# Placing x, the weights and the k order by their byte distances in SBUF in a two-layer hybrid block

## The chip, the core and the metric

The kernel runs on one core of one Trainium2 chip. The metric is the device time of one execution in microseconds, the median of the runs; the kernel before took 1326.98 us (median of 3 runs, 1326.49 to 1327.44). A smaller time is better.

## The reference

Two layers of a block on 256 tokens of width 1024, with 16 learned meta tokens in front (so T = 272). Each layer normalizes, projects to twelve parts, runs three branches (retention, a gated recurrence hgrn2, differential attention), mixes them through gates, and adds a gated feed-forward with a three-tap convolution:

```python
def mixer(hn, ...):
    proj = (hn @ w_in).astype(F32)                      # 1024 -> 13312
    o_ret = retention(rq, rk, rv, rg, ...); o_hg = hgrn2(...); o_da = diff_attention(...)
    y_b = jnp.einsum('blnc,ncd->blnd', branches, w_branch)   # three 1024x1024
    y = jnp.sum(jax.nn.sigmoid(mg) * y_b, axis=2)
    return y @ w_out                                     # 1024x1024

def conv_ffn(hn, ...):
    u = hn @ w_ffn_in                                    # 1024 -> 5632
    c = conv_b + sum(conv_w[j] * up[:, j:j + l] for j in range(3))
    gate, val = jnp.split(c, 2, axis=-1)
    return (jax.nn.silu(gate) * val) @ w_ffn_out         # 2816 -> 1024

for li in range(2):
    h = h + mixer(rms_norm(h, g_mix), ...)
    h = h + conv_ffn(rms_norm(h, g_ffn), ...)
return rms_norm(h, g_final)[:, PAD:]
```

Nearly all arithmetic is in the products of activations with weights.

## The kernel before, in words

Activations lie with features on the 128 partitions and tokens along them. A weight matrix is cut into tiles of 128 x 128, and one stream holds all tiles of both layers in the order of use. `_Weights.next` (L577) takes the stream in chunks of eight tiles: SP loads 512 KB into `wraw`, ACT copies it to `whi` (rounded to float32r), and DVE writes the remainder `wraw - whi` to `wlo`. Activations are split in the same way into a high and a low part. Each weight tile is then used in three matmuls, in this order (`products`, L873 to L875):

```python
nc.tensor.matmul(o, wh, hi, start=first, stop=False)
nc.tensor.matmul(o, wh, lo, start=False, stop=False)
nc.tensor.matmul(o, wl, hi, start=False, stop=last)
```

The weight tile is the operand that is loaded (128 columns of 4 bytes), the activation tile the one that moves. A moving tile has 272 columns, or 258 in those parts of the second layer that need no row of the meta tokens but the last two ("short"; `t0 = 14` moves its start by 56 bytes). L558 is the helper that records every other operation.

The stages of a layer, with the moving operand:

- **base**: the twelve projections, 52 pairs of output tiles, moving x. Six arrays hold x: `xs[0]`, `xs[1]`, `xs[2]`, each with a high and a low part. k tiles 0 to 3 come from `xs[0]`, or from `xs[2]` once the norm's factor is folded into x (from the fifth pair on), and k tiles 4 to 7 from `xs[1]`. In the second layer 22 of the 52 pairs run on all 272 columns (`FULL`), 30 are short.
- **blocks**: `b0`, `b1`, `b2` and `wo`, 16 pairs; the moving tiles lie in slots of 4 x 272 elements, so that one k tile begins 1088 bytes behind the other.
- **fi**: the feed-forward's first product, 22 pairs, moving x again.
- **fo**: its second product. In the first layer four pairs over 22 k tiles, moving `ghi` and `glo`; the fourth pair (`fo`, 3) takes all k of one output tile and then of the other. In the second layer `final` (L1351) turns the roles round: 512 columns of a weight chunk move, and 128 tokens of `ghi` or `glo` are loaded (L1383 to L1385).

A pair in base, blocks and fi is 8 k tiles x 2 output tiles x 3 = 48 matmuls; k is the outer loop of the two output tiles.

`_places` (L127) puts each weight tile of a chunk at a start that is fixed modulo 256 bytes, by the numbers in `APART` and, for fi, `SPREAD[j]`; gaps are left unused. Where a chunk's tiles don't lie in one run, `_runs` splits ACT's and DVE's work into pieces. What matters below is a **distance**: the start address of the operand that is loaded for the next matmul, less the start of the operand that moves in this one, modulo 256 bytes. By the addresses of the built program it is 64 in base on 272 columns, 104 in short base, 64 + `SPREAD[j]` in fi (another number for each pair), and in blocks and fo 64 (short: 104) but 128 (short: 168) where k goes up, which is one matmul in six.

A planner (`_Plan`) orders all instructions by costs and due times; it knows no addresses. `SLOTS` is the number of slots that it may hand out.

Of the kernel before, what the change touches and what calls it, by code (L numbers as in the profile page):

```python
# [19 lines left out]
P = 128  # L20
DEPTH = 2
# [13 lines left out]
TAIL = T - 2 * P  # L35
BANK = 512
CHUNK_TILES = 8
SLOTS = 13
LEAD = 6.0
MARGIN = 12.0  # L40
EARLY = 12.0
# [42 lines left out]
    return FK if name == "fo" else KD  # L84


def _turns(li):

    pairs = [x for x in ORDER if x[0][0] not in MARKS]
    if li == DEPTH - 1:
        pairs = [x for x in pairs if x[0] != "fo"]
    groups = [[x] for x in pairs]
    if li == 0:
        groups[:2] = [pairs[:2]]
    turned = [[x] for n in (BASE, ("fi",)) for x in [x for x in pairs if x[0] in n][DEFER - 1 : DEFER]]
    out = []
    for group in groups:  # L100
        if group == [("fo", 3)]:
            out.append([("fo", 3, k, f) for f in range(2) for k in range(FK)])
# [24 lines left out]
def _places(depth=DEPTH):  # L127

    wants = []
    for li in range(depth):
        for name, j, k, _ in sum(_turns(li), []):
            if name == "fo" and (li == DEPTH - 1 or j == 3):
                wants.append(None)
                continue
            short = li == DEPTH - 1 and name not in FULL
            if name in BASE or name == "fi":
                wants.append((SPREAD[j] + 4 * T0 * short if name == "fi" else APART[short]) % LINE)
                continue  # L140
            wants.append(APART[short] + BLOCK * (name[0] == "b" or name in ("wo", "fo")) + 64 * (k % 4))
    out = []
    for c in range(0, len(wants), CHUNK_TILES):
        at, places = 0, []
        for want in wants[c : c + CHUNK_TILES]:
            if want is not None:
                at += (want // 4 - at) % (LINE // 4)
            places.append(at)
            at += P
        assert at <= ROOM  # L150
        out.append(places)
    return out


def _runs(places):


    runs = []
    for i, at in enumerate(places):
        if runs and at == runs[-1][1] + runs[-1][2] * P:  # L160
            runs[-1][2] += 1
        else:
            runs.append([i, at, 1])
    out = []
    for i, at, n in runs:
        if out and out[-1][4] == n and (out[-1][3] == 1 or at == out[-1][1] + out[-1][2] * out[-1][3]):
            if out[-1][3] == 1:
                out[-1][2] = at - out[-1][1]
            out[-1][3] += 1
        else:  # L170
            out.append([i, at, 0, 1, n])
    return out


# [20 lines left out]
def _stream(w_in, w_branch, w_out, w_ffn_in, w_ffn_out):  # L195

    out = np.empty((DEPTH, STREAM, P, P), np.float32)
    for li in range(DEPTH):
        tiles = sum(_turns(li), [])
        for i, (name, j, k, f) in enumerate(tiles):  # L200
            if name in BASE:
                w, cols = w_in[li], _columns(name, BASE[name] + 2 * j + f)
            elif name in ("b0", "b1", "b2"):
                w, cols = w_branch[li][int(name[1])], _columns(name, 2 * j + f)
            elif name == "wo":
                w, cols = w_out[li], _columns(name, 2 * j + f)
# [6 lines left out]
    out = out.reshape(n, CHUNK_TILES, P, P).transpose(0, 2, 1, 3)  # L213
    return np.ascontiguousarray(out).reshape(n, P, CHUNK_TILES * P)


# [346 lines left out]
class _Weights:  # L563
# [6 lines left out]
        self.used = 0  # L570
        self.places = _places()

    def part(self, t, at, step, runs, n):

        return bass.AP(t.tensor, t.offset + at, [list(t.ap[0]), [max(step, 1), runs], [1, n * P]])

    def next(self):  # L577
        c, i = divmod(self.used, CHUNK_TILES)
        self.used += 1
        if i == 0:  # L580
# [7 lines left out]
            for p in range(pieces):  # L588
                n = CHUNK_TILES // pieces
                cols = slice(p * n * P, (p + 1) * n * P)  # L590
                self.sp.dma_start(raw[:, cols], self.w[c][:, cols])
                for first, at, step, runs, each in _runs(self.places[c][p * n : (p + 1) * n]):
                    src = raw[:, (p * n + first) * P : (p * n + first + runs * each) * P].rearrange("p (r x) -> p r x", r=runs)
                    self.act.activation(self.part(hi, at, step, runs, each), src, AF.Copy)
                    self.dve.tensor_tensor(out=self.part(lo, at, step, runs, each), in0=src, in1=self.part(hi, at, step, runs, each).bitcast(F32), op=SUB)
            self.plan.key = due
            self.cut = hi, lo
        hi, lo = self.cut
        at = self.places[c][i]
        return hi[:, at : at + P], lo[:, at : at + P]  # L600

    def chunk(self):

# [13 lines left out]
def _trace(ctx, tc, plan, a, depth, probe):  # L617
# [330 lines left out]
    for li in range(depth):  # L948
# [402 lines left out]
        def final():  # L1351
# [21 lines left out]
            for k, t, c in order:  # L1373
# [33 lines left out]
        for name, j in ORDER:  # L1407
# [111 lines left out]
                    norm.finish()  # L1519
            elif name == "fi":  # L1520
                ps = products(lambda k: x_tile(k, norm.folded), name, j, t0)
                if j % 4 == 0:
                    st.setdefault("ghi", []).append(slot4("ghi", F32R))
                    st.setdefault("glo", []).append(slot4("glo", F32R))
                u = ps
                if not norm.folded:
                    u = temp2("two_a")[:, :, t0:]
                    evacuate(u, ps)
                first = META if last else 0
                c = temp2("two_b")  # L1530
                for f in range(2):
                    ft = j + f * FK
# [9 lines left out]
                split(st["ghi"][j // 4][:, j % 4, first:], st["glo"][j // 4][:, j % 4, first:], c[:, 0, :])  # L1542
            elif last:
                if j == 0:
                    final()
# [37 lines left out]
```

## Time and profile before

| | before |
|---|---|
| median of 3 runs | 1326.98 us |
| the profiled execution | 1326.42 us |
| its span | 1324.6 us |
| TensorE matmul busy, matmuls | 1314.0 us, 11862 |
| TensorE weight load busy | 1285.7 us |
| VectorE (DVE) busy | 962.4 us |
| ScalarE (ACT) busy | 816.4 us |
| mean granted TensorE clock | 0.999 |

The span is the time between the first and the last instruction that the profiler saw. Busy times of one engine are sums over the span. A matmul's record lasts longer than the distance to the next one's start, since matmuls are pipelined: in a stretch that begins at a matmul's start, the count of matmuls holds two that had begun ahead of it. The pace of a stretch is therefore its length divided by the count less two.

### The profile page before, as it was taken

What the parts mean: (1) busy time and instruction counts of PE and PEld (TensorE: products, weight loads), DVE (VectorE), ACT (ScalarE), POOL (GpSimd) and SP (SyncE); (2) the same over time, 40 slices, a digit from 0 to 9 for tenths busy, and PEclk for the clock granted to TensorE, in tenths of its full rate; (3) what the DMA queues carried; (4) which work ended last, traced back from release to release, by engine and by line L of the source; (5) the groups of instructions that cost most, each with busy time, mean ns of one, the idle gap of its engine ahead of it and who ended that gap; (6) DMA issues with size and microseconds to landing.
All of it is one profiled execution on the core that took longest, in us unless ns stands there. A gap on an engine that the chain in (4) does not pass through costs nothing.

```text
span 1324.6 us, 28929 instructions
## 1 busy us (share of the span) xinstructions
PE 1314.0 (99%) x11862; PEld 1285.7 (97%) x11862; DVE 962.4 (73%) x1630; ACT 816.4 (62%) x1374; POOL 83.2 (6%) x161
## 2 busy tenths in 40 slices
PE   9999999999999999999999999999999999999998
PEld 8999999999999999999999999999999999999986
DVE  7675777697585789886574757776985867898753
ACT  6847454756576566666456475547565865766643
POOL 5000000001010020000030000000011100200000
PEclk9999999999999999999999999999999999999999
DMA  7544543444544545555555445444445345365653
GB/s 272 194 150 153 172 148 132 140 144 139 181 143 152 183 144 183 183 170 181 175 176 187 149 159 173 148 144 144 148 140 183 136 165 201 131 211 185 204 182 107
DMA packets 60755, 219.07 MB, mean 165 GB/s; under 512 B 6864, under 2 KB 6992, under 8 KB 60624
## 3 DMA queue, kind: packets, MB, share of 16 engines
q1 hardware_dynamic: 60336, 216.71, 48.0%
q8 instruction: 93, 1.52, 0.5%
q10 hardware_dynamic: 288, 0.52, 0.1%
q14 instruction: 38, 0.31, 0.1%
HBM read 216.16 MB, written 1.05 MB: 164 GB/s over the span
## 4 chain that ended last, share of the span: by engine, by line
PE 95%; DVE 3%; ACT 1%; issue 0%; DMA 0%; SPq 0%; DVEq 0%
PE main L873 28%; PE main L875 27%; PE main L874 27%; PE fo L1383 2%; PE fo L1385 2%; PE fo L1384 2%; PE lev L1064 1%; DVE two_b L558 1%; PE ds L1248 1%; PE ms L558 1%; PE do L558 1%; PE ro L558 1%; PE ho L558 1%; PE vt L558 1%; DVE wlo L558 1%; PE s L558 0%
## 5 line engine op out<-in xcount | busy, mean ns | idle before, releaser
L873 PE MATMUL main<-xh,whi 128*128 128x272 f32 (+1 forms) x2368 | 691.8, 292 | 0.7 <-ACT whi L558 0.7
L875 PE MATMUL main<-xh,wlo 128*128 128x272 f32 (+1 forms) x2368 | 676.1, 286 | 1.0 <-DVE wlo L558 0.9
L874 PE MATMUL main<-xl,whi 128*128 128x272 f32 (+1 forms) x2368 | 675.7, 285 | 1.3 <-DVE xl L558 1.3
L558 DVE TENSOR_TENSOR wlo<-wraw,whi 128x1024 fp32r<-128x1024 f32 (+1 forms) x408 | 497.2, 1223 | 197.9 <-ACT whi L558 195.2
L558 ACT ACTIVATE whi<-wraw 128x1024 fp32r<-128x1024 f32 (+1 forms) x408 | 426.4, 1048 | 228.1 <-PE main L874 160.1
L873 PEld LDWEIGHTS main<-xh,whi 128*128 128x128 f32 x2368 | 446.1, 188 | 2.6 <-ACT whi L558 1.1
L874 PEld LDWEIGHTS main<-xl,whi 128*128 128x128 f32 x2368 | 446.1, 188 | 2.3 <-DVE xl L558 1.7
L875 PEld LDWEIGHTS main<-xh,wlo 128*128 128x128 f32 x2368 | 445.7, 188 | 2.4 <-DVE wlo L558 2.3
L558 DVE SCALAR_TENSOR_TENSOR two_b<-main,small,two_b 128x256 f32<-128x256 f32 (+2 forms) x144 | 65.4, 489 | 30.7 <-ACT two_b L558 29.0
L558 ACT ACTIVATE two_b<-main,small 128x272 f32<-128x272 f32 (+1 forms) x72 | 37.2, 566 | 29.6 <-PE main L875 29.6
L558 POOL TENSOR_TENSOR y<-h,rstd 128x272 f32<-128x272 f32 x32 | 34.5, 1113 | 317.7 <-ACT rstd L558 317.7
L875 PE MATMUL main<-ghi,wlo 128*128 128x272 f32 x176 | 51.0, 290 | 0.0
L873 PE MATMUL main<-ghi,whi 128*128 128x272 f32 x176 | 50.9, 289 | 0.0
L874 PE MATMUL main<-glo,whi 128*128 128x272 f32 x176 | 50.2, 285 | 0.0
L558 ACT ACTIVATE vsrc<-main 128x544 f32<-128x544 f32 x24 | 15.0, 625 | 38.5 <-PE main L875 38.4
L873 PE MATMUL main<-b0hi,whi 128*128 128x272 f32 (+1 forms) x128 | 38.2, 298 | 0.0
L873 PE MATMUL main<-b1hi,whi 128*128 128x272 f32 (+1 forms) x128 | 38.1, 298 | 0.0
L875 PE MATMUL main<-b2hi,wlo 128*128 128x272 f32 (+1 forms) x128 | 36.7, 286 | 0.0
L875 PE MATMUL main<-yhi,wlo 128*128 128x272 f32 (+1 forms) x128 | 36.7, 286 | 0.0
L875 PE MATMUL main<-b1hi,wlo 128*128 128x272 f32 (+1 forms) x128 | 36.6, 286 | 0.0
L875 PE MATMUL main<-b0hi,wlo 128*128 128x272 f32 (+1 forms) x128 | 36.6, 286 | 0.0
L873 PE MATMUL main<-b2hi,whi 128*128 128x272 f32 (+1 forms) x128 | 36.5, 285 | 0.0
(244 smaller groups left out, 1934.4 us busy)
## 6 DMA issues: line engine op xcount, KB each, us to landing
wraw<-in_w SPq DMA_DIRECT2D x402, 512.0 KB, 3.3
h<-in_h SPq DMA_DIRECT2D x4, 272.0 KB, 5.7
dec<-in_dec SPq DMA_DIRECT2D x2, 544.0 KB, 5.5
wraw<-in_w SPq DMA_DIRECT2D x4, 256.0 KB, 5.4
const<-in_const SPq DMA_DIRECT2D x1, 937.0 KB, 6.4
gain<-in_gl SPq DMA_DIRECT2D x1, 512.0 KB, 5.2
out<-y ACTq DMA_DIRECT2D x2, 256.0 KB, 2.8
out<-y SPq DMA_DIRECT2D x2, 256.0 KB, 2.7
```

The source lines that it names most:

```text
L558: self.plan.add(self.name, lambda: f(*args, **kw), cost, outs, ins, args[2] if method == "activation" else None)
L873: nc.tensor.matmul(o, wh, hi, start=first, stop=False)
L874: nc.tensor.matmul(o, wh, lo, start=False, stop=False)
L875: nc.tensor.matmul(o, wl, hi, start=False, stop=last)
L1064: nc.tensor.matmul(o, keys, x, start=True, stop=True)
L1248: nc.tensor.matmul(ss[m][:, at : at + nk], q[half, hd, q0 : q0 + P], k[half, hd, :nk], start=True, stop=True)
L1383: nc.tensor.matmul(o, gh, wh, start=False, stop=False)
L1384: nc.tensor.matmul(o, gl, wh, start=False, stop=False)
L1385: nc.tensor.matmul(o, gh, wl, start=False, stop=end)
```

## The change

Nothing is computed otherwise, and the multiplications are the same. Five things move:

- x lies in two tiles instead of six: `x01` holds, for each k tile, the high part for k < 4, its low part, the high part for k >= 4, and its low part, 1088 bytes apart, so one k tile begins 4352 bytes (17 x 256) behind the last; `x2` holds a high and a low part 1088 bytes apart with rows of 2304 bytes (9 x 256).
- `whi` and `wlo` get places of their own in a chunk: 64 bytes (short: 160 bytes) behind the moving tile of the matmul during which they load, modulo 256. The tiles of a chunk may be laid out in another order than that of use (`order`), and the stream in HBM is written in that order.
- blocks and fo take k downward in blocks of four: 3, 2, 1, 0, 7, 6, 5, 4 (`wo`: 3, 2, 1, 0, 5, 4, 7, 6).
- In the second layer `ghi` and `glo` leave out the meta tokens, so a k tile has 1024 bytes.
- `SLOTS` is 14.

```diff
-SLOTS = 13
+SLOTS = 14
+def _ks(name):
+    ks = list(range(_ktiles(name)))
+    if name in BASE or name == "fi":
+        return ks
+    blocks = [ks[i : i + 4][::-1] for i in range(0, len(ks), 4)]
+    if name == "wo":
+        blocks[-1] = [5, 4, 7, 6]
+    return sum(blocks, [])
...
-            out.append([x + (k, f) for k in range(nk // 2) for x in group for f in range(2)])
-            out[-1] += [x + (k, f) for x in group for k in range(nk // 2, nk) for f in range(2)]
+            ks = _ks(group[0][0])
+            out.append([x + (k, f) for k in ks[: nk // 2] for x in group for f in range(2)])
+            out[-1] += [x + (k, f) for x in group for k in ks[nk // 2 :] for f in range(2)]
...
-APART = (0, 96)
+BEGIN = 64
-ROOM = CHUNK_TILES * P + 2 * LINE // 4
+LATE_X = 2 * T + 32
+ROOM = CHUNK_TILES * P + LINE // 4
-SPREAD = [16 * i for i in range(16)] + [8 + 40 * i for i in range(6)]
-WIDE = 320
+APART = (64, 160)
...
             if name in BASE or name == "fi":
-                wants.append((SPREAD[j] + 4 * T0 * short if name == "fi" else APART[short]) % LINE)
-                continue
-            wants.append(APART[short] + BLOCK * (name[0] == "b" or name in ("wo", "fo")) + 64 * (k % 4))
+                moving = [4 * T * (2 * (k >= 4) + part) for part in range(2)]
+            else:
+                moving = [BLOCK + 4 * T * (k % 4)] * 2
+            wants.append([APART[short] + 4 * T0 * short - BEGIN + x for x in moving])
...
+        if c // CHUNK_TILES > 1 and None not in mine:
+            order.sort(key=lambda i: mine[i][0] % LINE)
+        for part in range(2):
+            at = 0
+            for i in order:
+                if mine[i] is not None:
+                    at += (mine[i][part] // 4 - at) % (LINE // 4)
+                places[part][i] = at
+                at += P
...
-    xs = [[fixed([P, KD // 2, WIDE], f"x{n}{i}", F32R)[:, :, :T] for n in "hl"] for i in range(3)]
+    both = fixed([P, KD // 2, 4, T], "x01", F32R)
+    late = fixed([P, KD // 2, LATE_X], "x2", F32R)
+    xs = [[both[:, :, 2 * i + n, :] for n in range(2)] for i in range(2)]
+    xs.append([late[:, :, n * T : (n + 1) * T] for n in range(2)])
...
-                gh, gl = (x[k // 4][:, k % 4, tokens(t)] for x in (hi, lo))
+                gh, gl = (x[k // 4][:, k % 4, t * P : (t + 1) * P] for x in (hi, lo))
...
+                first = META if last else 0
                 if j % 4 == 0:
-                    st.setdefault("ghi", []).append(slot4("ghi", F32R))
-                    st.setdefault("glo", []).append(slot4("glo", F32R))
+                    for n in ("ghi", "glo"):
+                        g = slot(n, F32R)[:, : 4 * (T - first)]
+                        st.setdefault(n, []).append(g.rearrange("p (a t) -> p a t", a=4))
```

`_boxes` takes the place of `_runs`: it joins the tiles of a chunk into as few regular two-level patterns as fit `whi` and `wlo` alike, one instruction of ACT and one of DVE for each.

The distances by the built program's addresses (the smaller number of cases in brackets):

| stage | before | after |
|---|---|---|
| base, 272 columns | 64 | 64 (192 twice in 48 matmuls, where k passes from one half of x to the other) |
| base, short | 104 | 160 (32 twice in 48) |
| fi, first layer | 64 + `SPREAD[j]` | 64 (192 twice in 48) |
| fi, second layer | 64 + `SPREAD[j]` | 160 (32 twice in 48) |
| blocks and fo, first layer | 64 (128 once in 6) | 64 (0 once in 6) |
| blocks, second layer | 104 (168 once in 6) | 160 (96 once in 6) |
| (`fo`, 3) | 0, 64, 128, 192 in turn | 64 (0 once in 3) |
| final | 64, 128, 192, 0 in turn | 0 |

What moves in a row is little. On PE the rows stand in the same order before and after, stage by stage; only the names of x differ. Five of them from the first base pairs before, the three matmuls of one weight tile and two of the next (`xh0` and `xl0` are the high and the low part of `xs[0]`):

```order
L873 MATMUL main_37_112<-xh0_14_89,whi1_117 128x272
L874 MATMUL main_37_112<-xl0_15_90,whi1_117 128x272
L875 MATMUL main_37_112<-xh0_14_89,wlo1_118 128x272
L873 MATMUL main_36_111<-xh0_14_89,whi1_117 128x272
L874 MATMUL main_36_111<-xl0_15_90,whi1_117 128x272
```

and at the same place after (both parts are in `x01` now):

```order
L908 MATMUL main_33_108<-x01_14_89,whi1_113 128x272
L909 MATMUL main_33_108<-x01_14_89,whi1_113 128x272
L910 MATMUL main_33_108<-x01_14_89,wlo1_114 128x272
L908 MATMUL main_32_107<-x01_14_89,whi1_113 128x272
L909 MATMUL main_32_107<-x01_14_89,whi1_113 128x272
```

The instructions are the same; the low part began 5120 bytes (20 x 256) behind the high one and now begins 1088 bytes (64 modulo 256) behind it, and `wlo` has moved with it by 64 against `whi`. So a weight tile's distance to its own moving tile, which was 64 in all three matmuls, is 64, 0 and 128 in them now, while the distance to the tile that moves while it loads stays 64.

On ACT (and in the same way on DVE) the pieces of some chunks differ, all in fo of the first layer. Before, at the end of fo there:

```order
L558 ACTIVATE whi195_1213<-wraw195_1212 128x4x256
L558 ACTIVATE whi196_1216<-wraw196_1215 128x256
L558 ACTIVATE whi196_1216<-wraw196_1215 128x768
L558 ACTIVATE whi197_1222<-wraw197_1221 128x1024
L558 ACTIVATE whi198_1225<-wraw198_1224 128x1024
```

After:

```order
L589 ACTIVATE whi195_1209<-wraw195_1208 128x4x256
L589 ACTIVATE whi196_1212<-wraw196_1211 128x2x128
L589 ACTIVATE whi196_1212<-wraw196_1211 128x2x256
L589 ACTIVATE whi196_1212<-wraw196_1211 128x2x128
L589 ACTIVATE whi197_1218<-wraw197_1217 128x4x256
L589 ACTIVATE whi198_1221<-wraw198_1220 128x4x256
```

Chunk 196 is in three pieces instead of two. Over the whole program ACT and DVE have three instructions more each; POOL's and SP's rows are the same in kind and order.

More of the change, by code (lines that the diff above doesn't have):

```diff
@@ L142, in _places @@
     out = []
     for c in range(0, len(wants), CHUNK_TILES):
[L144 to L151, printed above, removed]
-    return out
[L155 to L171, printed above, removed]
+        mine = wants[c : c + CHUNK_TILES]
@@ new lines, in _places @@
+        order, places = list(range(CHUNK_TILES)), [[0] * CHUNK_TILES for _ in range(2)]
+        if c // CHUNK_TILES > 1 and None not in mine:
[7 more added lines that the diff above has]
+                at += P
+            assert at <= ROOM, at
+        out.append((order, places))
@@ new lines, in _places, with _boxes, box @@
+    return out
+def _boxes(*places):
+    def box(first, n):
+        for inner in (n, 2, 1):
+            if n % inner:
+                continue
+            dims = []
+            for at in places:
+                at = at[first : first + n]
+                one = at[1] - at[0] if inner > 1 else P
+                two = at[inner] - at[0] if inner < n else 0
+                if one < 1 or two < 0 or any(at[i] != at[0] + i // inner * two + i % inner * one for i in range(n)):
+                    break
+                dims.append((at[0], two, one))
+            if len(dims) == len(places):
+                return first, n // inner, inner, dims
+        return None
+    out, first, end = [], 0, len(places[0])
+    while first < end:
+        found = next(x for n in range(end - first, 0, -1) if (x := box(first, n)))
+        out.append(found)
+        first += found[1] * found[2]
@@ L571, in __init__, with part @@
         self.places = _places()
-    def part(self, t, at, step, runs, n):
-        return bass.AP(t.tensor, t.offset + at, [list(t.ap[0]), [max(step, 1), runs], [1, n * P]])
+    def part(self, t, at, two, one, outer, inner):
+        return bass.AP(t.tensor, t.offset + at, [list(t.ap[0]), [max(two, 1), outer], [one, inner], [1, P]])
     def next(self):
```

26 lines of the change are left out of this document (14 added, 12 removed).

## The prediction

> **What bounds the kernel now.** I read the page first: busy times, granted clock, and the shares of the chain that ended last.
>
> ```profile
> span 1324.6 us, 28929 instructions
> PE 1314.0 (99%) x11862; PEld 1285.7 (97%) x11862; DVE 962.4 (73%) x1630; ACT 816.4 (62%) x1374; POOL 83.2 (6%) x161
> PEclk9999999999999999999999999999999999999999
> PE 95%; DVE 3%; ACT 1%; issue 0%; DMA 0%; SPq 0%; DVEq 0%
> L873 PE MATMUL main<-xh,whi 128*128 128x272 f32 (+1 forms) x2368 | 691.8, 292 | 0.7 <-ACT whi L558 0.7
> L558 DVE TENSOR_TENSOR wlo<-wraw,whi 128x1024 fp32r<-128x1024 f32 (+1 forms) x408 | 497.2, 1223 | 197.9 <-ACT whi L558 195.2
> ```
>
> TensorE is busy for 99% of the span at its full clock and makes 95% of the chain. A busy PE may still be a waiting one, so I looked at who PE waited for.
>
> ```profile
> PE main L874 <- DVE xl L558: 1.3, 1, 1.3
> PE warm L558 <- POOL ones_d L558: 1.0, 1, 1.0
> PE main L875 <- DVE wlo L558: 0.9, 4, 0.3
> PE main L873 <- ACT whi L558: 0.7, 2, 0.5
> PE wt L558 <- DVE two_a L558: 0.2, 1, 0.2
> ```
>
> That is the whole list, 4.1 us. The span is thus a sum of matmul paces, and a change that leaves every engine's order alone can only act through the pace. So I cut the span into stretches that each hold one distance, starting and ending at a matmul's start. The columns are length, then busy time and count of PE, PE's loads, DVE, ACT and POOL, clock, and DMA. First layer: base, blocks, the early and the late part of fi, then fi pairs with distances 0, 72, 112 and 152.
>
> ```profile
> 38.38:73.90 35.52, 35.52 (x290) 35.52 (x289) 21.89 (x43) 25.09 (x31) 0.00 (x0) 1.00 0.63 208
> 425.61:449.55 23.94, 23.94 (x194) 23.94 (x193) 15.61 (x17) 14.18 (x14) 0.00 (x0) 1.00 0.53 177
> 473.50:529.17 55.67, 55.35 (x436) 54.66 (x435) 50.98 (x82) 40.47 (x65) 8.47 (x8) 1.00 0.48 163
> 529.17:607.61 78.44, 78.44 (x626) 78.44 (x625) 63.51 (x106) 50.95 (x78) 0.00 (x0) 1.00 0.53 176
> 547.25:553.26 6.01, 6.01 (x50) 6.01 (x49) 4.88 (x9) 3.92 (x6) 0.00 (x0) 1.00 0.53 168
> 571.41:577.35 5.94, 5.94 (x50) 5.94 (x49) 4.74 (x9) 3.92 (x6) 0.00 (x0) 1.00 0.49 167
> 577.35:583.43 6.08, 6.08 (x50) 6.08 (x49) 5.03 (x9) 3.92 (x6) 0.00 (x0) 1.00 0.55 179
> 583.43:589.55 6.12, 6.12 (x50) 6.12 (x49) 4.91 (x9) 3.92 (x6) 0.00 (x0) 1.00 0.52 171
> ```
>
> Two matmuls of each count had begun earlier. Base, all at distance 64, runs at 35.52 / 288 = 123.3 ns a matmul. The four fi pairs, 48 matmuls each of the same shape with the same work around them, run at 125.2 (distance 0), 123.8 (72), 126.7 (112) and 127.5 (152). Late fi as a whole: 78.44 / 624 = 125.7. Blocks, at 64 but for one jump to 128 in six: 23.94 / 192 = 124.7, so a jump costs (124.7 - 123.3) x 6 = **8.1 ns**.
>
> Second layer: base on 272, short base, blocks, early fi, fi at 160 (the second half of that pair), 176, 0, and late fi.
>
> ```profile
> 685.92:706.65 20.73, 20.73 (x170) 20.73 (x169) 14.47 (x16) 13.21 (x15) 2.63 (x7) 1.00 0.57 187
> 712.45:732.23 19.78, 19.78 (x170) 19.78 (x169) 10.14 (x10) 11.29 (x13) 0.00 (x0) 1.00 0.57 186
> 1080.61:1103.60 22.99, 22.99 (x194) 22.99 (x193) 15.36 (x17) 13.88 (x14) 0.00 (x0) 1.00 0.53 183
> 1126.58:1169.07 42.49, 41.17 (x340) 40.88 (x339) 39.07 (x64) 31.59 (x51) 8.63 (x8) 1.00 0.44 155
> 1166.27:1169.07 2.80, 2.80 (x26) 2.80 (x25) 2.80 (x7) 1.37 (x2) 0.00 (x0) 1.00 0.84 279
> 1169.07:1174.88 5.81, 5.81 (x50) 5.81 (x49) 5.18 (x10) 3.95 (x7) 0.00 (x0) 1.00 0.47 159
> 1197.84:1203.60 5.76, 5.76 (x50) 5.76 (x49) 4.91 (x10) 3.79 (x6) 0.00 (x0) 1.00 0.61 206
> 1169.07:1252.50 83.43, 83.43 (x698) 83.43 (x697) 69.77 (x120) 56.96 (x90) 0.00 (x0) 1.00 0.60 199
> ```
>
> On 258 columns: distance 104 gives 19.78 / 168 = 117.7, 160 gives 2.80 / 24 = 116.7, 176 gives 121.0, 0 gives 120.0, late fi 83.43 / 696 = 119.9. Blocks run at 22.99 / 192 = 119.7, so a jump costs (119.7 - 117.7) x 6 = **12.0 ns**. Last the final product: 19 of its 22 k tiles, then one k tile at 64 and one at 0.
>
> ```profile
> 1257.12:1309.75 52.63, 52.63 (x230) 42.87 (x229) 25.67 (x25) 23.07 (x24) 0.00 (x0) 1.00 0.49 169
> 1268.19:1270.99 2.80, 2.80 (x13) 2.26 (x12) 1.22 (x1) 1.09 (x2) 0.00 (x0) 1.00 0.57 196
> 1276.53:1279.26 2.73, 2.73 (x13) 2.25 (x12) 1.23 (x1) 1.05 (x2) 0.00 (x0) 1.00 0.51 192
> ```
>
> The whole runs at 52.63 / 228 = 230.8 ns, 64 at 2.80 / 12 = 233.3 and 0 at 227.5. (A record there reaches over one earlier or two, by the counts; I took 12 per k tile from the code.)
>
> [...]
>
> **The change part by part.** The sum takes late stages at the pace of the new distance, plus jumps; matmul counts are from the loops.
>
> 1. Base on 272 columns (104 + 44 chunks of 24 matmuls) stays at 64 and gets one jump to 192 per chunk. No row shows a single jump to 192; I take the 8.1 ns of 128: 148 x 8.1 = **+1.2 us** (bounds 0 and +2.4).
> 2. Late fi, first layer: 123.3 + 8.1 / 24 = 123.7 against 125.7, times 624: **-1.3**.
> 3. Early fi there (432 matmuls in 55.67 us): at 123.7 it would take 53.4. But DVE is busy for 50.98 of it, and a faster PE waits for DVE sooner. I take half: **-1.1** (0 to -2.2).
> 4. Short base, 1440 matmuls: 117.7 to 116.7 is -1.5; 60 jumps to 32, priced like 168's at 12.0, are +0.7: **-0.8** (-1.5 to 0).
> 5. Blocks, second layer, 768: 116.7 + 2.0 = 118.7 against 119.7: **-0.8** (-2.4 with free jumps, +0.7 with doubled ones).
> 6. Late fi, second layer, 720: 116.7 + 0.5 = 117.2 against 119.9: **-1.9**. DVE has 69.77 us of work in 83.43 and would have it in 81.6, so it keeps up.
> 7. Early fi there, 336: 42.49 us against 39.4; DVE's 39.07 us nearly fill that. A third: **-1.0** (0 to -3.1).
> 8. Final, 264: 227.5 against 230.8: **-0.9**.
> 9. Blocks and fo of the first layer keep 64 and trade the jump to 128 for one to 0. With the same price that is **0**; free jumps would give -1.6, doubled ones +1.6. (`fo`, 3), 144 matmuls, is small.
>
> The other edits cost nothing. No PE row moves, so no wait is added. Taking k downward asks for no operand earlier than it is ready: b0 to b2 split all four k tiles of a slot at once, `wo` still ends on k 7 and 6, and fo takes k 21 last or last but one. The three more pieces on DVE come in first-layer fo, of which this is a stretch:
>
> ```profile
> 607.61:631.55 23.94, 23.94 (x194) 23.94 (x193) 14.07 (x19) 12.92 (x17) 0.00 (x0) 1.00 0.56 192
> ```
>
> DVE rests there for 9.9 of 23.9 us, and three pieces are at most 3 x 1.2 us by their row on the page; if that cover were gone, PE's next `wlo` would come late by one piece. DMAs keep sizes and order. A fourteenth slot changes nothing while the order is the same.
>
> Sum: 1.2 - 1.3 - 1.1 - 0.8 - 0.8 - 1.9 - 1.0 - 0.9 = **-6.6 us**. The profiled execution took 1326.42 us, so 1319.8 for its like; it lay 0.6 under the median, so **1320.4** beside the median.
>
> **The rivals.**
>
> *The other distance counts as well (slower).* A weight tile stood 64 bytes from its own moving tile in all three matmuls; now it is 64, 0, 128. If the pace depends on that, where one matmul ends and the next begins, base loses its 123.3. At 126.7, the row for 112, 3552 matmuls cost +12.1 us and terms 2 and 3 are gone (+2.4): 1320.4 + 14.5 = 1334.9. It turns the sign once base is 1.9 ns slower. Against it: the pace follows the new distance within a few matmuls at each fi pair, whatever the pair before had. For it: before, the two distances differ only in jumps, and those cost 8 to 12 ns.
>
> *Jumps cost double and early fi gives nothing (about the same).* +2.1 for terms 3 and 7, and +1.2, +0.4, +0.7, +0.5, +1.5 for the jumps of terms 1, 2, 4, 6, 5: 1326.8.
>
> *Jumps are free (faster still).* -1.2 - 0.4 - 0.7 - 0.5 - 1.5 - 1.6: 1314.5.
>
> *Placement does nothing*, and the paces of fi come from something else, such as DVE's writes: 1327.0. [...] The rows speak against it: DVE has 4.74 to 5.03 us in those fi pairs, and at 1166.27 it is busy throughout while PE runs its best pace.
>
> **How the numbers follow.** Chances: forecast 0.57, other distance 0.15, double jumps 0.13, free jumps 0.11, nothing 0.04. The range 1314.5 to 1328.0 takes in free jumps below and double jumps above; the slower rival is left out. A measurement of this kernel tells about 0.2% from no change, so faster means under 1324.3 and slower over 1329.6. Faster: nearly all of the forecast and of free jumps, 0.67. Same: double jumps, nothing, and some mild form of the slower rival, 0.21. Slower: 0.12.
>
> **What would show it.** Right: late fi at 123.7 and 117.2 ns, final at 227, short base near 117.2, base still at 123.3 plus a third of a nanosecond, PE's waits a few microseconds. Wrong: a base above 125 (the other distance), early fi as long as before with more waits for `wlo` or `xl` (DVE takes the gain), or blocks of the first layer away from 124.7 (the jump's price).

## The result, and the profile after

The changed kernel takes **1328.4 us** (median of 21 runs, 1326.43 to 1329.8) against 1326.3 (21 runs, 1325.74 to 1327.44) for the kernel before: ratio 1.0016, 95% interval 1.0009 to 1.0022. It is slower by about 2 us. The interval lies above 1, but the step is smaller than the 0.2% that the prediction took as its bound for telling a change from none. The forecast was 1320.4, 8 us away. A part of the gain came and was paid away elsewhere, and the rest did not come.

The page of the changed kernel, its first lines, the chain, and the costliest group:

```profile
span 1326.3 us, 28932 instructions
...
PE 1316.1 (99%) x11862; PEld 1288.7 (97%) x11862; DVE 963.0 (73%) x1633; ACT 817.0 (62%) x1377; POOL 84.0 (6%) x161
...
PE 94%; DVE 4%; issue 1%; ACT 1%; DMA 0%; SPq 0%; DVEq 0%; ACTq 0%
...
L908 PE MATMUL main<-x,whi 128*128 128x272 f32 (+1 forms) x2368 | 690.0, 291 | 0.1
```

The span is 1.7 us longer and PE is busy for 2.1 us more; DVE and ACT are as busy as before. All that PE waited for:

```profile
PE main L909 <- DVE x L589: 1.5, 1, 1.5
PE warm L589 <- POOL ones_d L589: 1.0, 1, 1.0
PE main L910 <- DVE wlo L589: 0.7, 3, 0.3
PE wt L589 <- DVE two_a L589: 0.2, 1, 0.2
```

That is 3.4 us against 4.1. No wait was added, so, as forecast, the change acts through the pace of matmuls alone. The stretches of the prediction, cut at the same matmuls in the changed kernel (columns as there). First layer: base, blocks, early fi, late fi, fo; second layer: base on 272, short base, blocks, early fi, late fi, final.

```profile
38.15:74.35 36.20, 36.20 (x290) 36.20 (x289) 21.77 (x43) 24.97 (x31) 0.00 (x0) 1.00 0.62 203
429.47:453.30 23.83, 23.83 (x194) 23.83 (x193) 15.61 (x17) 14.16 (x14) 0.00 (x0) 1.00 0.54 177
477.17:532.89 55.72, 55.33 (x436) 54.63 (x435) 50.49 (x82) 40.46 (x65) 8.46 (x8) 1.00 0.49 162
532.89:611.33 78.44, 78.44 (x626) 78.44 (x625) 64.19 (x106) 51.00 (x78) 0.00 (x0) 1.00 0.53 176
611.33:635.17 23.84, 23.84 (x194) 23.84 (x193) 14.13 (x19) 12.92 (x17) 0.00 (x0) 1.00 0.57 193
689.30:710.39 21.09, 21.09 (x170) 21.09 (x169) 14.52 (x16) 13.21 (x15) 2.62 (x7) 1.00 0.55 188
716.22:736.07 19.85, 19.85 (x170) 19.85 (x169) 10.15 (x10) 11.31 (x13) 0.00 (x0) 1.00 0.56 186
1085.42:1108.01 22.59, 22.59 (x194) 22.59 (x193) 15.45 (x17) 13.91 (x14) 0.00 (x0) 1.00 0.56 185
1130.75:1173.15 42.40, 40.78 (x340) 40.26 (x339) 39.07 (x64) 31.54 (x51) 8.63 (x8) 1.00 0.46 152
1173.15:1255.40 82.25, 82.25 (x698) 82.25 (x697) 69.50 (x120) 56.87 (x90) 0.00 (x0) 1.00 0.62 203
1259.99:1311.69 51.70, 51.70 (x230) 42.80 (x229) 25.62 (x25) 23.08 (x24) 0.00 (x0) 1.00 0.50 172
```

Base kept its distance of 64 and yet went from 35.52 to 36.20 us (125.7 ns a matmul instead of 123.3) and, in the second layer, from 20.73 to 21.09. Late fi of the first layer is exactly as long as before (78.44 us), although all its pairs now stand at the distance of base. Short base is 19.85 against 19.78, although it went to 160, where the kernel before had its best pace on 258 columns. On the other side the second layer's blocks went from 22.99 to 22.59, its late fi from 83.43 to 82.25, and final from 52.63 to 51.70.

What separates base from what it was is visible inside a weight tile's three matmuls. In the first layer's base of the changed kernel the mean time from a matmul's start to the next start is 124.4 ns for the first (`hi`, `whi`), 127.0 for the second (`lo`, `whi`) and 125.2 for the third (`hi`, `wlo`), leaving out distances over 160 ns; in the kernel before it is 123.4, 123.8 and 123.9. The weight tile's place against its own moving tile is 64, 0 and 128 in these three.

### The profile page after: what moved, and what is told of

It is laid out like the page before. It is cut to its first block, busy times and chain, and to the rows that moved or that the text cites. A ratio compares the mean times of both kernels' runs of the same rounds, so it can differ in the third digit from the quotient of the medians.

```text
span 1326.3 us, 28932 instructions
## 1 busy us (share of the span) xinstructions
PE 1316.1 (99%) x11862; PEld 1288.7 (97%) x11862; DVE 963.0 (73%) x1633; ACT 817.0 (62%) x1377; POOL 84.0 (6%) x161
## 4 chain that ended last, share of the span: by engine, by line
PE 94%; DVE 4%; issue 1%; ACT 1%; DMA 0%; SPq 0%; DVEq 0%; ACTq 0%
PE main L908 27%; PE main L909 27%; PE main L910 27%; PE fo L1420 2%; PE fo L1419 2%; PE fo L1418 2%; PE lev L1099 1%; DVE two_b L589 1%; PE ds L1283 1%; DVE wlo L589 1%; PE ms L589 1%; PE do L589 1%; PE ro L589 1%; PE ho L589 1%; PE vt L589 1%
## 5 line engine op out<-in xcount | busy, mean ns | idle before, releaser
L908 PE MATMUL main<-x,whi 128*128 128x272 f32 (+1 forms) x2368 | 690.0, 291 | 0.1
L909 PE MATMUL main<-x,whi 128*128 128x272 f32 (+1 forms) x2368 | 679.0, 287 | 1.5 <-DVE x L589 1.5
L910 PE MATMUL main<-x,wlo 128*128 128x272 f32 (+1 forms) x2368 | 677.2, 286 | 1.0 <-DVE wlo L589 0.7
L909 PEld LDWEIGHTS main<-x,whi 128*128 128x128 f32 x2368 | 447.5, 189 | 2.5 <-DVE x L589 1.9
L908 PEld LDWEIGHTS main<-x,whi 128*128 128x128 f32 x2368 | 445.4, 188 | 2.1 <-issue 0.3
L910 PEld LDWEIGHTS main<-x,wlo 128*128 128x128 f32 x2368 | 444.8, 188 | 2.6 <-DVE wlo L589 2.5
L908 PE MATMUL main<-yhi,whi 128*128 128x272 f32 (+1 forms) x128 | 36.4, 284 | 0.0
L909 PE MATMUL main<-b0lo,whi 128*128 128x272 f32 (+1 forms) x128 | 36.4, 284 | 0.0
L909 PE MATMUL main<-b1lo,whi 128*128 128x272 f32 (+1 forms) x128 | 36.4, 284 | 0.0
```

## The experiments

**Theory A:** a weight tile has to stand right both to the tile that moves while it loads and to the tile that moves with it; in other words, each change of the moving tile's start (modulo 256) from one matmul to the next costs time, and the low part's 64 bytes make two such changes in every three matmuls. (In the kernel before, the load for the matmul that starts at 49.98 us stands at 49.86 to 50.05 us, beside the matmul that starts at 49.85.) **Theory B:** only the few jumps between the halves of x cost, at more than the prediction's price. **Theory C:** something else, such as one shared tile for both parts of x or the other pieces on ACT and DVE.

### x in six arrays that begin alike

The changed kernel with the low part beginning where the high part does, modulo 256. Everything else of the change stays (fi at one distance, k downward, short `ghi`).

```diff
-SLOTS = 14
+SLOTS = 13
-                moving = [4 * T * (2 * (k >= 4) + part) for part in range(2)]
+                moving = [0, 0]
-    both = fixed([P, KD // 2, 4, T], "x01", F32R)
-    late = fixed([P, KD // 2, LATE_X], "x2", F32R)
...
+    xs = [[fixed([P, KD // 2, 320], f"x{n}{i}", F32R)[:, :, :T] for n in "hl"] for i in range(3)]
```

> The changed kernel, but high and low parts and all k tiles of x begin alike modulo 256 (six arrays of 320 columns, 13 slots), so each weight tile stands 64 (short: 160) bytes both from the tile that moves while it loads and from its own, and base and fi have no jumps. Theory A (the offset between high and low part costs the pace): base back to 123.3 ns, fi at 123.3 and 116.7, short base near 116.7; by stages -8.9 us against before, about 1317.5 us. Theory B (only the jumps between the halves of x cost): the paces away from jumps are what they were in the changed kernel, 125.5 and 118.2, and 1326 us. Theory C (something else of the change, such as the shared tile of x or the pieces on ACT and DVE, slows base): no faster than the changed kernel, 1328 us.

Measured: **1317.8 us** (1317.55 to 1321.05), ratio 0.994 (0.9928 to 0.9953). This is faster than both kernels, and the best one of the study. Its span is 1315.7 us. Its stretches, in the order of the list above, without fo:

```profile
37.83:73.35 35.52, 35.52 (x290) 35.52 (x289) 21.88 (x43) 25.07 (x31) 0.00 (x0) 1.00 0.63 207
425.01:448.85 23.84, 23.84 (x194) 23.84 (x193) 15.61 (x17) 14.15 (x14) 0.00 (x0) 1.00 0.55 177
472.71:528.04 55.33, 54.60 (x436) 53.88 (x435) 50.49 (x82) 40.44 (x65) 8.47 (x8) 1.00 0.49 163
528.04:605.00 76.96, 76.96 (x626) 76.96 (x625) 64.05 (x106) 50.90 (x78) 0.00 (x0) 1.00 0.57 179
...
682.84:703.56 20.72, 20.72 (x170) 20.72 (x169) 14.51 (x16) 13.21 (x15) 2.69 (x7) 1.00 0.57 187
709.33:728.93 19.60, 19.60 (x170) 19.60 (x169) 10.12 (x10) 11.33 (x13) 0.00 (x0) 1.00 0.60 187
1075.90:1098.46 22.56, 22.56 (x194) 22.56 (x193) 15.44 (x17) 13.90 (x14) 0.00 (x0) 1.00 0.55 188
1121.21:1163.48 42.27, 40.51 (x340) 39.96 (x339) 38.96 (x64) 31.50 (x51) 8.62 (x8) 1.00 0.46 151
1163.48:1244.68 81.20, 81.20 (x698) 81.20 (x697) 69.56 (x120) 56.84 (x90) 0.00 (x0) 1.00 0.62 206
1249.24:1300.93 51.69, 51.69 (x230) 42.80 (x229) 25.61 (x25) 23.08 (x24) 0.00 (x0) 1.00 0.51 173
```

Base is back at 35.52 us, late fi falls to 76.96 (123.3 ns) and 81.20 (116.7 ns), and the three matmuls of a weight tile in the first base now take 123.4, 123.9 and 123.8 ns. Blocks and final, where no low part was moved, are as in the changed kernel. ACT and DVE have the changed kernel's pieces here (1633 and 1377 instructions in both), so the pieces are not the cause. This run undoes the offset and the jumps between the halves at once; the next two part them.

### The offset without the jumps

The changed kernel with the low part 64 bytes behind, but all halves of x beginning alike.

```diff
-                moving = [4 * T * (2 * (k >= 4) + part) for part in range(2)]
+                moving = [4 * T * part for part in range(2)]
-    both = fixed([P, KD // 2, 4, T], "x01", F32R)
...
+    for i in range(3):
+        wide = fixed([P, KD // 2, LATE_X], f"x{i}", F32R)
+        xs.append([wide[:, :, n * T : (n + 1) * T] for n in range(2)])
```

> The changed kernel with three tiles of x in place of two: the low part still begins 64 bytes behind the high one modulo 256, but both halves of k begin alike, so the jumps to 192 and 32 in base and fi are gone. Theory A: base stays at 125.3 to 125.5 ns and fi at 125.3 and 118.0; only the jumps' cost goes, about 148 x 8 ns and 104 x 5 ns, so 1326.5 us. Theory B: base at 123.3, fi at 123.3 and 116.7, 1318 us.

Measured: 1326.42 us (1324.59 to 1331.29), ratio 1.0004 (0.9994 to 1.0014). Base of the first layer, late fi of the first layer, base on 272 of the second:

```profile
38.93:75.09 36.16, 36.16 (x290) 36.16 (x289) 21.75 (x43) 24.86 (x30) 0.00 (x0) 1.00 0.62 204
533.22:611.56 78.34, 78.34 (x626) 78.34 (x625) 63.70 (x106) 50.95 (x78) 0.00 (x0) 1.00 0.56 175
689.50:710.60 21.10, 21.10 (x170) 21.10 (x169) 14.52 (x16) 13.21 (x15) 2.63 (x7) 1.00 0.56 189
```

The loss is all there without a jump. B is out. (By stages this trace is 0.2 us shorter than that of the changed kernel, 1214.74 against 1214.95, and the runs scatter over 7 us, so what the jumps cost is not read from here.)

### The jumps without the offset

The first experiment with the second half of x 128 bytes further on.

```diff
-                moving = [0, 0]
+                moving = [128 * (k >= 4)] * 2
-    xs = [[fixed(...)[:, :, :T] for n in "hl"] for i in range(3)]
+    xs = [[fixed(...)[:, :, 32 * (i == 1) : 32 * (i == 1) + T] for n in "hl"] for i in range(3)]
```

> High and low part alike as in the first kernel of this call, but the second half of k begins 128 bytes behind the first, so that the jumps to 192 (short: 32) are there without the offset between high and low. Theory A: paces of 123.3 and 116.7 away from jumps, a jump in 24 matmuls at some 8 and 10 ns: about 1.9 us over the first kernel, 1319.5 us. Theory B: like the changed kernel, 1327 to 1328 us.

Measured: 1319.51 us (1318.81 to 1320.52), ratio 0.9946 (0.9931 to 0.9962). Base of the first layer, and short base:

```profile
38.22:73.82 35.60, 35.60 (x290) 35.60 (x289) 21.90 (x43) 25.07 (x31) 0.00 (x0) 1.00 0.65 207
710.81:730.43 19.62, 19.62 (x170) 19.62 (x169) 10.11 (x10) 11.31 (x13) 0.00 (x0) 1.00 0.60 185
```

With the jumps alone base loses 0.08 us in 288 matmuls, 12 jumps. Over all base and fi stages the jumps cost 1.14 us; 148 pairs with two jumps each make that **3.9 ns a jump**. The prediction priced them at 8.1 and 12.0. By the medians they cost 1319.5 - 1317.8 = 1.7 us, as Theory A had it.

This is also the layout that the prediction priced: one distance, jumps, and nothing else. It takes 1319.5 us where 1320.4 was forecast for the change.

### A map of the pace, with no other engine at work

This kernel leaves out the whole computation: 8352 matmuls of 272 and 258 columns back to back, in stretches of one distance each, every matmul with its own load. It was meant to rule C in or out.

> This kernel leaves out the whole computation: it loads some data and runs 8352 matmuls of 128 x 128 on 272 or 258 columns back to back, in stretches of one distance each (0 to 248 in steps of 8, upward, then downward for both sizes), then with a low part offset by 16 to 224 bytes at the distances 64 and 160, then with a shift of all addresses once in 12 matmuls and in each one, the distance to the tile that moves kept. Theory A: stretches of one distance repeat the levels of fi (123.3 at 64, 116.7 at 160), an offset of 64 gives 125.5 and 118.2, and each shift costs one or two matmuls some ns although the distance stays. If distance to the moving tile alone decided, offsets and shifts would leave 123.3 and 116.7. If other engines' accesses made the levels of fi, all stretches would be alike here.

Its time, 1063.25 us, means nothing by itself. On 272 columns, 48 matmuls a stretch: distances 64, 0, 112, 152; then distance 168 twice, once with the distances going up and once with them going down; then 72 matmuls at 64 whose second of three has its moving tile 64 bytes further on, and 72 each in which every moving tile lies 64, and then 192, bytes further on than the one before, modulo 256; last 258 columns at distance 160, the moving tile at a multiple of 64 bytes. (Two or three of each count had begun before.)

```profile
79.43:85.35 5.92, 5.92 (x50) 5.92 (x49) 0.00 (x0) 0.00 (x0) 0.00 (x0) 1.00 0.00 0
779.29:785.31 6.02, 6.02 (x50) 6.02 (x49) 0.00 (x0) 0.00 (x0) 0.00 (x0) 1.00 0.00 0
695.28:701.36 6.08, 6.08 (x51) 6.08 (x50) 0.00 (x0) 0.00 (x0) 0.00 (x0) 1.00 0.01 3
145.62:151.76 6.14, 6.14 (x50) 6.14 (x49) 0.00 (x0) 0.00 (x0) 0.00 (x0) 1.00 0.00 0
157.78:163.70 5.92, 5.92 (x50) 5.92 (x49) 0.00 (x0) 0.00 (x0) 0.00 (x0) 1.00 0.00 0
653.11:659.19 6.08, 6.08 (x50) 6.08 (x49) 0.00 (x0) 0.00 (x0) 0.00 (x0) 1.00 0.00 0
803.44:812.50 9.06, 9.06 (x74) 9.06 (x73) 0.00 (x0) 0.00 (x0) 0.00 (x0) 1.00 0.01 2
1020.30:1029.38 9.08, 9.08 (x74) 9.08 (x73) 0.00 (x0) 0.00 (x0) 0.00 (x0) 1.00 0.00 0
1029.38:1038.39 9.01, 9.01 (x75) 9.01 (x73) 0.00 (x0) 0.00 (x0) 0.00 (x0) 1.00 0.01 2
339.35:345.11 5.76, 5.76 (x51) 5.76 (x49) 0.00 (x0) 0.00 (x0) 0.00 (x0) 1.00 0.01 3
```

DVE, ACT and POOL stand at 0.00, DMA next to nothing, and the paces are those of fi before: 123.3 ns at 64 (5.92 / 48; 123.3 in base before), 125.4 at 0 (125.2), 126.7 at 112 (126.7), 127.9 at 152 (127.5). The levels are there with no other engine at work, and between these stretches only the addresses differ, so here they come from the addresses on PE. Within a stretch the starts differ by multiples of 256 bytes only (1280 from one k tile that moves to the next, 512 and 16384 among the loaded tiles), and at 64 the 48 matmuls keep 123.3 ns. All moving tiles of the map lie in one SBUF tile, so a shared tile does not make the loss either; C is out. With the low part's offset the stretch at 64 goes from 123.3 to 9.06 / 72 = 125.8 ns, base of the changed kernel to a tenth of a nanosecond. All eight offsets that the map tried, 16 to 224 bytes, cost something there: 124.5 ns (at 96, 128 and 160) to 126.7 (at 16).

Single changes of the start show little in the mean. Where all addresses shift by 64 bytes once in twelve matmuls the mean is 123.48 ns instead of 123.29 (about 2 ns a shift), by 128 it is 123.61 (about 4), by 192 123.72 (about 5). Two changes in three matmuls, as base has them, come to (125.8 - 123.3) x 3 / 2 = 3.7 ns each, and a change at every matmul to 126.1 - 123.3 = 2.8 ns each for 64 and 1.8 for 192. So there is no single price for a change, but each of these has one, and it was there whichever distance was kept: in the map's shifts the distance of the next load to the moving tile stays at 64, and the weight tile's distance to its own moving tile changes; in the jumps of x and of the blocks it is the other way round. A change by 128 cost some 4 ns in both (x, 3.9), by 192 some 5 in both (the blocks downward, (124.2 - 123.3) x 6), and by 64 it cost 2 in the map and 8 in the blocks upward.

Two rows did not fit. At distance 168 the same matmuls ran at 123.3 ns on the way up and at 126.7 on the way down. And 258 columns at 160 ran at 120.0, while fi of the kernel before ran its pair at 160 at 116.7; the offset of 64 left it at 120.0 (8.64 us for 72) where Theory A had said 118.2. The kernel's short tiles begin 56 bytes behind a multiple of 64, those of the map on it.

### k upward again

The first experiment with the order of k as before, to price what the other direction brings.

```diff
 def _ks(name):
-    ks = list(range(_ktiles(name)))
-    if name in BASE or name == "fi":
-        return ks
-    blocks = [ks[i : i + 4][::-1] for i in range(0, len(ks), 4)]
-    if name == "wo":
-        blocks[-1] = [5, 4, 7, 6]
-    return sum(blocks, [])
+    return list(range(_ktiles(name)))
```

> This is e1_alike with every product taking k upward again, so that a block's moving tiles jump to 128 (short: 224) where it jumps to 0 (short: 96) in e1. Theory A (the pace depends on each operand's place against the tile that moves while it loads and on the tile's own): the direction of k is worth what the traces show for the two jumps, so the first layer's blocks and fo go back to 124.6 and 124.7 ns (+0.4 us together) and the second layer's blocks, whose jump to 224 no run has shown, lie between 118.2 and 119.7 ns (0 to +1.2 us): 1318.2 to 1319.4 us, ratio to the kernel before 0.9942 to 0.9952. Rival (the direction of k does something else too, such as the order in which operands come free): PE's waits grow, and the time is over 1320.

Measured: 1320.4 us (1319.22 to 1321.37), ratio 0.9954 (0.9941 to 0.9966): 2.6 us over the first experiment, above the range of Theory A and just inside its rival's. Blocks of the first layer, blocks of the second:

```profile
425.32:449.27 23.95, 23.95 (x194) 23.95 (x193) 15.61 (x17) 14.18 (x14) 0.00 (x0) 1.00 0.55 177
1077.36:1100.24 22.88, 22.88 (x194) 22.88 (x193) 15.35 (x17) 13.91 (x14) 0.00 (x0) 1.00 0.57 185
```

The first layer's blocks are back at 124.7 ns (23.94 us in the kernel before). The second layer's take 22.88 us in this stretch against 22.56, and 94.16 over the whole stage against 92.81: 120.0 ns on average against 118.2. By the rows, which hold no other work of PE, the jump to 224 costs (119.2 - 116.7) x 6 = 15 ns, and the jump to 96 that the downward order makes (117.5 - 116.7) x 6 = 5. The stages add up to +1.8 us and the spans of the two profiled executions differ by 1.9, so the paces explain the difference of the traces; Theory A's range failed in its upper end, 119.7 ns as the stage's average with a jump that no run had shown. The 0.7 us by which the medians differ beyond that is within the two intervals. PE waits 0.7 us once for a `whi` in the first 400 us, as in the kernel before and not in the first experiment; that is too little for the rival. Without the downward order, moving short weights to 160 would have gained nothing in the blocks (93.88 us before).

### fi's weights alone, in the kernel before

```diff
-                wants.append((SPREAD[j] + 4 * T0 * short if name == "fi" else APART[short]) % LINE)
+                wants.append((APART[short] + 4 * T0 * short if name == "fi" else APART[short]) % LINE)
```

> This is the kernel before with fi's weights alone moved, to 64 (first layer) and 160 (second) in all pairs; x stays in its six arrays, k upward, base and blocks as before. Theory A: fi runs as in e1_alike, 55.1, 77.0, 42.0 and 84.1 us against 55.4, 78.4, 42.2 and 86.4 in the kernel before, which is -4.4 us, and nothing else moves: 1321.9 us, ratio 0.9967. Rival (the pace of e1_alike comes from its fewer pieces on ACT and DVE or from its one row of 320 columns for all parts of it together): fi gains less than half of this, over 1324 us.

Measured: 1322.02 us (1321.4 to 1323.63), ratio 0.9972 (0.996 to 0.9983). Base, late fi of the first layer, late fi of the second, final:

```profile
38.13:73.65 35.52, 35.52 (x290) 35.52 (x289) 21.90 (x43) 25.16 (x31) 0.00 (x0) 1.00 0.63 208
528.76:605.72 76.96, 76.96 (x626) 76.96 (x625) 63.84 (x106) 50.90 (x78) 0.00 (x0) 1.00 0.56 178
1166.94:1248.14 81.20, 81.20 (x698) 81.20 (x697) 69.57 (x120) 56.77 (x90) 0.00 (x0) 1.00 0.63 204
1252.74:1305.37 52.63, 52.63 (x230) 42.88 (x229) 25.66 (x25) 23.07 (x24) 0.00 (x0) 1.00 0.54 170
```

1321.9 was expected. One line of the change, by itself, gives 4 us; late fi has the first experiment's length to the last digit, and base and final have that of the kernel before.

### A second map: short tiles at their real place, and final's shape

Again the whole computation is left out. 258 columns begin 56 bytes behind a multiple of 64, and matmuls of 512 columns are added.

> It leaves out the whole computation: matmuls back to back with no other engine at work. Those of 258 columns begin 56 bytes behind a multiple of 64, as the kernel's short ones do, at each distance in steps of 8, once upward and once downward; then with the second of three moved by an offset; and those of 512 columns at each distance in steps of 16. If the moving tile's place modulo 64 is what set e4_map's 258 columns apart from the kernel, distance 160 gives 116.7 ns here (120.1 there) and 104 gives 117.5, and an offset of 64 at 160 gives 118.2, as in the changed kernel's short base. If it is something else in the kernel, 160 gives 120 again. For 512 columns the kernel shows 226.7 to 227.5 ns at distance 0 and 230 to 233 at 64: if placement makes these, the map shows them, with no other engine working.

258 columns at distance 128, at 160, and at 160 with the offset of 64 (72 matmuls); then 512 columns (36 matmuls) at 0, 64, 128 and 192:

```profile
123.30:129.96 6.66, 6.66 (x50) 6.66 (x49) 0.00 (x0) 0.00 (x0) 0.00 (x0) 1.00 0.00 0
147.26:152.87 5.61, 5.61 (x50) 5.61 (x49) 0.00 (x0) 0.00 (x0) 0.00 (x0) 1.00 0.01 3
418.11:426.59 8.48, 8.48 (x74) 8.48 (x73) 0.00 (x0) 0.00 (x0) 0.00 (x0) 1.00 0.01 2
675.40:683.56 8.16, 8.16 (x38) 6.76 (x37) 0.00 (x0) 0.00 (x0) 0.00 (x0) 1.00 0.00 0
708.51:716.91 8.40, 8.40 (x38) 6.77 (x36) 0.00 (x0) 0.00 (x0) 0.00 (x0) 1.00 0.00 0
742.08:750.48 8.40, 8.40 (x37) 6.76 (x36) 0.00 (x0) 0.00 (x0) 0.00 (x0) 1.00 0.00 0
775.55:783.79 8.24, 8.24 (x37) 6.76 (x36) 0.00 (x0) 0.00 (x0) 0.00 (x0) 1.00 0.01 2
```

At 160 it is 5.61 / 48 = 116.9 ns now, with the offset 8.48 / 72 = 117.8: the 56 bytes are what set the first map apart (120.0 there), and the offset's price is seen here too (0.9 ns a matmul; short base of the changed kernel: 118.2). Distance 104, expected at 117.5, gave 121.1 on the way up and 117.7, once settled, on the way down: right one way and wrong the other, and another distance with two paces. For final: 226.7 at 0, 233.3 at 64, 233.3 at 128, 228.9 at 192. Their mean is 230.6; final in the kernel before, which goes through the four in turn, runs at 230.8.

## Why the prediction was wrong

Time by stage, as the sum over the starts of the products' matmuls in each trace, in us; in brackets the mean distance of two starts, leaving out those over 160 ns. "Six arrays" is the first experiment.

| stage | before | after | six arrays | forecast | after, measured |
|---|---|---|---|---|---|
| base on 272, both layers | 454.73 (123.7) | 460.14 (125.5) | 454.01 (123.7) | +1.2 | +5.4 |
| late fi, first layer | 78.44 (125.7) | 78.43 (125.7) | 76.96 (123.3) | -1.3 | 0.0 |
| early fi, first layer | 55.42 (125.4) | 55.47 (125.3) | 55.07 (123.5) | -1.1 | 0.0 |
| short base | 177.15 (118.5) | 177.22 (118.5) | 175.78 (117.5) | -0.8 | +0.1 |
| blocks, second layer | 93.88 (119.7) | 92.84 (118.2) | 92.81 (118.2) | -0.8 | -1.0 |
| late fi, second layer | 86.39 (119.9) | 85.17 (118.2) | 84.10 (116.7) | -1.9 | -1.2 |
| early fi, second layer | 42.23 (120.4) | 42.14 (118.2) | 42.02 (117.3) | -1.0 | -0.1 |
| final | 60.71 (230.9) | 59.64 (226.8) | 59.62 (226.7) | -0.9 | -1.1 |
| blocks and fo, first layer | 164.44 | 163.90 | 163.89 | 0 | -0.5 |
| sum | 1213.39 | 1214.95 | 1204.26 | -6.6 | +1.6 |

**The step that failed** is the first one, "base on 272 columns stays at 64", priced with jumps alone, and with it the pace of every stage that moves x. The forecast let the pace depend on one distance only, that of the load to the tile moving meanwhile. The text under the order rows, ahead of the prediction, said that the other distance goes from 64, 64, 64 to 64, 0, 128, and the prediction named this as a rival ("the other distance counts as well") with a chance of 0.15. The experiments show that it is what happened: with the offset and no jumps the loss is all there, with the jumps and no offset it is gone and the gain in late fi comes. The layout with jumps alone is the forecast's own picture, and its stages add up to -8.0 us and its median lies 6.7 us under that of the kernel before (-6.6 forecast): base -0.2, late fi -1.3 and -2.2, short base -1.1, blocks and final of the second layer -1.0 and -1.1. That the sum comes so near is partly luck, since jumps in base that were too dear (+1.2) and early fi that was too rich (-2.1 forecast, -0.5 there) take each other off. The rival's size was too large: it took 126.7 ns, the row for distance 112, where the changed kernel shows 125.5, so its 1334.9 lies 6.5 us too high.

The prediction had a hint and booked it one way only. In the blocks' jumps (8 ns once in six matmuls) the moving tile's start changes and the weight tile keeps its own distance, so the price could belong to the distance to the next load or to the change itself. A layout that changes the start twice in three matmuls had to be priced for the second case too, at that rate, and not at nothing because the loads keep their distance. The argument "the pace follows the new distance within a few matmuls at each fi pair" showed that the first distance matters; it said nothing about the second. It does not hold everywhere either: in the maps some distances keep two paces, by what ran before.

Term by term otherwise:

- **Late fi (terms 2 and 6), short base (4):** the mechanism was right and the size would have been, for the layout with equal starts: -1.5, -2.3 and -1.4 in the first experiment against -1.3, -1.9 and -0.8 forecast. In the changed kernel the offset takes back all of it on 272 columns (125.7 again) and in short base, and half of it in the second layer's late fi.
- **Blocks of the second layer (5), final (8):** right in size, -1.0 and -1.1 against -0.8 and -0.9. For the blocks that is partly luck: the jump to 96 was priced at 12.0 ns and costs 5, so `b2` fell by 2 ns a matmul and not by 1, but `wo`, whose order of k still makes two jumps to 224 in eight, fell by 1.2 (118.5 ns on average), and `b0` and `b1`, with other work of PE in between, by about 1. Final had its price from one k tile's row, and the second map confirms it without any other engine.
- **Blocks and fo of the first layer (9):** put at 0 with the same price for the jump to 0 as for that to 128; by the rows the jump to 0 is cheaper by (23.94 - 23.83) / 32, some 3 ns: -0.5 in all, 0.1 of it in (`fo`, 3).
- **Early fi (3 and 7):** too large even where the pace did fall. Two things went wrong. First, the whole stretch was divided by its pace, although 55.42 - 432 x 0.1254 = 1.3 us of the first one and 1.8 us of the second are waits and other work in between, which no pace of the products shortens; 0.8 and 1.0 us were to be had, not 2.2 and 3.1. Second, PE's idle time grew: in the first experiment PE is busy for 54.60 of 55.33 us (55.35 of 55.67 before) and 40.51 of 42.27 (41.17 of 42.49), DVE for 50.49 and 38.96; the longest wait of all, for `xl` in the second of them, went from 1.3 to 1.7 us. That left 0.35 and 0.2 us there, and 0.0 and 0.1 in the changed kernel. The rival's half, "early fi gives nothing", was nearly right.
- **Price of a jump:** 8.1 and 12.0 ns were taken from jumps of other sizes. Between the halves of x it is 3.9 on average; in the second layer's blocks 5 (to 96) or 15 (to 224). There is no one price.
- **The edits put at nothing** (a fourteenth slot, three more pieces on DVE and ACT, the order of k on readiness) cost nothing that shows: PE's waits shrank from 4.1 to 3.4 us.
- **"Placement does nothing"** is refuted by both maps: with nothing but PE at work, 48 matmuls of 272 columns took 5.92 us at distance 64 and 6.14 at 152, and 48 of 258 columns took 5.61 at 160 and 6.66 at 128. What makes them slower there, no run shows.

## What to carry to other kernels

Here, where each matmul brings its own weights (11862 loads for 11862 matmuls) and PE is hardly ever idle (99% busy, 3.4 to 4.1 us of waits), the start addresses modulo 256 of both operands were worth up to 4% of a matmul of 272 columns (123.3 to 127.9 ns), and a map of 8352 matmuls with nothing else running gave the table. What paid here was to let all moving tiles of a stage begin alike and to choose one weight distance for them, by the number of columns and the place of the moving tile (64 for 272 columns, 123.3 ns; 160 for 258 columns that begin 56 bytes behind a multiple of 64, 116.7): changing the start by 64 bytes and back in every three matmuls cost as much (125.8 ns) as a middling distance (125.4 at 0). When a layout keeps one relation between two addresses, write down the other ones and price those that change, at the rate at which they change.

## What the runs showed that was not expected

- **Two paces at one distance.** 272 columns at 168 ran at 123.3 and at 126.7 ns, 258 columns at 104 at 121.1 and 117.7, each steady once settled and differing only in what ran before. These were not the only ones: 272 columns at 144 ran at 126.7 (6.08 us for 48) and, once settled, at 123.4, 512 columns at 16 at 226.7 and 233.3. So the pace of these stretches hung on how they were entered, and one row of this map is not yet a pace.
- **The start of the moving tile counted too.** 258 columns at distance 160: 120.0 ns with the moving tile on a multiple of 64, 116.9 with it 56 bytes behind.
- **A deep hole.** 258 columns at distance 128, 56 behind: 6.66 us for 48. The first three to five starts are 117 to 125 ns apart, all the others exactly 140, 20% over the best pace. On a multiple of 64 the same distance gave 120.0 and 122.2.
- **A jump was not paid where it happened.** In the map's stretch with a shift of 64 once in twelve, the distances of the starts behind the shift are 121, 125, 126.7, 122 ns and then level off: the second and third matmul are the long ones.

Left open: why one distance is slower than another; which of the things that the low part's offset changes at once costs the pace (with a fixed distance to the next load, each weight tile's distance to its own moving tile changes, and the starts of moving and loaded tiles alternate; no run parts these); why the 56 bytes matter (120.0 against 116.9 ns); and what a layout without any jump in the blocks would bring. With starts 1280 bytes apart in their slots too, the paces above would give some 2 us, an estimate from (124.2 - 123.3) x 1.3 thousand and (117.5 - 116.7) x 0.77 thousand matmuls of the rows' paces; it was not tried.
